# GpSimd's additions in a kernel's first stage turned into adding transfers

## The chip, the cores and the metric

The kernel runs on one core of one Trainium2 chip. The time is the device time of one launch in microseconds, lower is better. The core has five engines that run at the same time, each taking its own instructions strictly in order: TensorE (matmuls and transposes, PE in the profile, its weight loads PEld), VectorE (DVE), ScalarE (ACT), GpSimd (POOL) and SyncE (SP), which here only issues transfers. 16 DMA engines move data between HBM and the on-chip buffer SBUF; a transfer is issued from the queue of SP, of ScalarE or of GpSimd, and an instruction that needs its data waits on a semaphore until it has landed. Matmul results go to PSUM, from which DVE and ACT read them.

## What is computed

A decoder trunk of two layers on 1024 tokens of width 1024, all float32. The first layer is a gated MLP whose gate mixes tokens within chunks of 128, the second a Mamba-2 mixer. Only the beginning matters here: the RMS norm of the input, and the product of the normed tokens with the part `v` of the first layer's input weights:

```python
hn = rmsnorm(h, norm_w[i])
z, u, v = jnp.split(h @ w_in, 3, axis=-1)      # h is hn here
v = layernorm(v, ln_w, ln_b)
```

## The kernel before

**Matmuls.** A float32 value is split in a high part `hi` (rounded to float32r by ScalarE's copy) and a low part `lo` (the rest, by a subtraction on VectorE); a product is three matmuls, hi·hi, lo·hi, hi·lo (`mm3`, lines 131 to 136).

**Strassen blocks.** `Block` (from line 182) computes a product X·W with X cut in halves by tokens and by input columns (A11, A12, A21, A22) and W in four blocks `b[0,0]`, `b[1,0]`, `b[0,1]`, `b[1,1]`. Instead of eight block products there are seven, numbered 1 to 7, of sums of blocks: on the side of the tokens S1 to S4, on the side of the weights t1 = b01 − b00, t2 = b11 − t1, b11 − b01 (written over b01) and b10 − t2 (written over b10). Product 1 takes A11 and b00, 2 takes A12 and b10, 3 takes S4 and b11, 4 takes A22 and b10 − t2, 5 takes S1 and t1, 6 takes S2 and t2, 7 takes S3 and b11 − b01. A product has two units of 24 matmuls (`blk.mm(n, i)`), each for two tiles of 128 tokens; tiles 0 to 3 are token half 1, tiles 4 to 7 token half 2. `blk.post` reads a finished accumulator.

**The head.** `head` (lines 345 to 533) is the first stage. Under `manual_schedule` each engine runs its instructions in the order in which they are written. SP loads eight rows of tokens (`load_x`; row t is 128 tokens by 1024 columns, 512 KB) and the four blocks of weights (`blk.load`, 512 KB each; row 7 takes the buffer of b00 and so waits until b00 has been read for the last time). For each row ScalarE sums squares (`sq`); `rs_a` has VectorE scale them and GpSimd raise them to −1/2 (line 141); `rs_b` makes four small VectorE operations of it (lines 150 to 153); `norm` scales the row (line 376); `tr` transposes it on TensorE into PSUM; `hi` and `lo` split it into A11, A12 or A22 (lines 391 and 395), and `copy` (line 398) keeps an unsplit copy in the row's own buffer, `F[t][:, kh]` with kh the half of the columns. `yhi` and `ylo` (lines 402 and 405) split weights.

From the copies come the tokens' sums. `s3(t)`: F[t−4][:,0] −= F[t][:,0]. `s1(t)`: F[t][:,0] += F[t][:,1]. `s2(t)`: F[t][:,1] −= F[t−4][:,0] as s3 left it. `s4(t)`: F[t−4][:,1] −= F[t][:,1] as s2 left it. Of tiles 0 to 3 only the first half of the columns is copied; the second is made again from the split (`again`, hi + lo). GpSimd does the weights' four sums (lines 452, 453, 459, 460), s3 of tiles 4 to 6, s1 of tiles 4 to 6, `again`, s4 of tiles 5 to 7 and two `ylo`; GpSimd also does s3 of tile 7; VectorE does s2 of all four tiles, s1 of tile 7 and s4 of tile 4. All these are `tensor_tensor` instructions.

The products come in the order 1 and 2 of tokens half 1, unit 0; unit 1; then 4, 6, 7, 5, 3, and then the second block (`nxt`), whose weights `nxt.load` fetches into buffers as they come free, and whose sums VectorE makes. Product 3 adds onto product 5's accumulator, so it starts when `blk.post(5, ...)` has read that.

**An idiom that is there already.** `Block.add` (line 197) adds a block of weights from HBM onto a tile in SBUF by a transfer with `accum_op=ALU.add`, issued from GpSimd's queue (line 202); later blocks use it (`sums_a`, `sums_b`, `fourth`: ScalarE's `mul` by −1 at lines 211, 212, 217, 227, then adds), and line 1089 adds 512 KB from SBUF to SBUF. Two adds onto the same tile wait for one another.

Of the kernel before, what the change touches and what calls it, by code (L numbers as in the profile page):

```python
# [8 lines left out]
F32 = mybir.dt.float32  # L9
F32R = mybir.dt.float32r  # L10
AF = mybir.ActivationFunctionType
ALU = mybir.AluOpType
# [10 lines left out]
G = 8  # L23
# [6 lines left out]
def kernel(  # L30
# [21 lines left out]
    nc = tc.nc  # L52
    x = x[0]
    out = out[0]
# [22 lines left out]
    def tiny(shape, name):  # L77
        return sb.tile(shape, F32, name=name, tag="tiny", bufs=8)
# [103 lines left out]
    class Block:  # L182
# [139 lines left out]
    def v_block(gp):  # L322
        def done(name, i, a, b):
            th, j = int(name[1]) - 1, int(name[2]) - 1
            g = 2 * gp + j
            vt = k2([P, 2, 256], "vt")
            vf = vt.rearrange("p a b -> p (a b)")
            if b is None:
                nc.scalar.copy(out=vf, in_=a)
            else:  # L330
                nc.vector.tensor_tensor(out=vf, in0=a, in1=b, op=ALU.add)  # L331
            t0 = th * 4 + 2 * i
            for q in range(2):
                nc.vector.bn_stats(out=stats[:, t0 + q, g, :], in_=vt[:, q, :])
            (nc.gpsimd if gp else nc.sync).dma_start(out=v_d[g][:, t0:t0 + 2, :], in_=vt)

        def W(kh, j):
            c = 2 * DI + (2 * gp + j) * 256
            return [a_w_in[kh * 512:(kh + 1) * 512, c:c + 256]]

        return Block(HS, W, True, done)
# [3 lines left out]
    def head():  # L345

        blk = v_block(0)
        V, S, G = nc.vector, nc.scalar, nc.gpsimd
        TTv, TTg = V.tensor_tensor, G.tensor_tensor
        rows, F, TP, ss, rs = {}, {}, {}, {}, {}  # L350

        def load_x(t, dst):
# [4 lines left out]
        def sq(t):  # L357
            if t % 2 == 0:
                ss[t] = tiny([P, 8], "ss")
            junk = HS["S4"][t // 2 % 2][:, t % 2 * 2:t % 2 * 2 + 2].rearrange("p a b -> p (a b)")  # L360
            S.activation(junk, rows[t], AF.Square, accum_out=ss[t // 2 * 2][:, t % 2:t % 2 + 1])
# [24 lines left out]
        def part(name, t):  # L386
            sl = slice(t % 4 * P, (t % 4 + 1) * P)
            return [m[:, :, sl] for m in HS[name]]

        def hi(name, t, src):  # L390
            S.copy(out=part(name, t)[0], in_=src)

        def lo(name, t, src):
            h_, l_ = part(name, t)
            TTv(out=l_, in0=src, in1=h_.bitcast(F32), op=ALU.subtract)  # L395

        def copy(t, kh):
            S.copy(out=F[t][:, kh], in_=TP[t][kh])

        def yhi(n, src, eng=S.copy):  # L400
            blk.Y[n] = (wh([P, 4, 256]), wl([P, 4, 256]))
            eng(out=blk.Y[n][0], in_=src)

        def ylo(n, src, eng=TTv):
            eng(out=blk.Y[n][1], in0=src, in1=blk.Y[n][0].bitcast(F32), op=ALU.subtract)  # L405

        def again(t):

            h_, l_ = part("A12", t)
            TTg(out=F[t][:, 1], in0=h_.bitcast(F32), in1=l_.bitcast(F32), op=ALU.add)  # L410

        def s3(t):
            TTg(out=F[t - 4][:, 0], in0=F[t - 4][:, 0], in1=F[t][:, 0], op=ALU.subtract)

        def s1(t, eng):
            eng(out=F[t][:, 0], in0=F[t][:, 0], in1=F[t][:, 1], op=ALU.add)

        def s2(t):
            TTv(out=F[t][:, 1], in0=F[t][:, 1], in1=F[t - 4][:, 0], op=ALU.subtract)

        def s4(t, eng=TTg):
            eng(out=F[t - 4][:, 1], in0=F[t - 4][:, 1], in1=F[t][:, 1], op=ALU.subtract)

        b = blk.b
        t1, t2 = q4([P, 4, 256], "t1"), q4([P, 4, 256], "t2")
# [14 lines left out]
        for o, ap in ((0, a_ln_w), (16, a_ln_b), (32, b_norm_w), (48, b_conv_b)):  # L440
            n = ap.shape[1] // P
# [1 line left out]

        sq(0), sq(1), rs_a(0), rs_b(0), sq(2)
        norm(0), tr(0), norm(1), tr(1)
        hi("A11", 0, TP[0][0]), copy(0, 0), sq(3), hi("A12", 0, TP[0][1])
        rs_a(2), yhi(1, b[0, 0], V.tensor_copy)
        lo("A11", 0, TP[0][0]), ylo(1, b[0, 0]), lo("A12", 0, TP[0][1]), rs_b(2)
        hi("A11", 1, TP[1][0]), copy(1, 0), hi("A12", 1, TP[1][1])
        lo("A11", 1, TP[1][0]), lo("A12", 1, TP[1][1])  # L450
        yhi(2, b[1, 0]), ylo(2, b[1, 0])
        TTg(out=t1, in0=b[0, 1], in1=b[0, 0], op=ALU.subtract)
        TTg(out=t2, in0=b[1, 1], in1=t1, op=ALU.subtract)
        blk.mm(1, 0, False), sq(4), blk.post(1, 0), sq(5)
        blk.mm(2, 0, False)
        norm(2), tr(2), norm(3), tr(3)
        rs_a(4), rs_b(4), norm(4)
        hi("A11", 2, TP[2][0]), copy(2, 0), hi("A12", 2, TP[2][1])
        TTg(out=b[1, 0], in0=b[1, 0], in1=t2, op=ALU.subtract)
        TTg(out=b[0, 1], in0=b[1, 1], in1=b[0, 1], op=ALU.subtract)  # L460
        lo("A11", 2, TP[2][0]), lo("A12", 2, TP[2][1])
        hi("A11", 3, TP[3][0]), copy(3, 0), hi("A12", 3, TP[3][1])
        lo("A11", 3, TP[3][0]), lo("A12", 3, TP[3][1])
        norm(5)
        blk.mm(1, 1, False, (0,)), tr(4), blk.mm(1, 1, False, (1,))
        blk.mm(2, 1, False, (0,)), tr(5), blk.mm(2, 1, False, (1,))
# [2 lines left out]
        copy(4, 0), rs_a(6), blk.post(2, 0), rs_b(6)  # L469
        hi("A22", 5, TP[5][1]), copy(5, 1), copy(5, 0), blk.post(1, 1)  # L470
        lo("A22", 5, TP[5][1]), norm(6), norm(7)
        for t in (4, 5):
            s3(t), s1(t, TTg)
        yhi(6, t2)
        blk.mm(4, 0, False, (0,)), tr(6), blk.mm(4, 0, False, (1,)), tr(7)
        hi("A22", 6, TP[6][1]), copy(6, 1), copy(6, 0)
        lo("A22", 6, TP[6][1]), blk.post(2, 1), ylo(6, t2)
        hi("A22", 7, TP[7][1]), copy(7, 1), copy(7, 0)
        lo("A22", 7, TP[7][1])
        s3(6), s1(6, TTg), s3(7)  # L480
        blk.mm(4, 1, False)
        yhi(7, b[0, 1]), ylo(7, b[0, 1], TTg)
        for t in (4, 5):
            s2(t), hi("S2", t, F[t][:, 1])
        for t in (4, 5):
            lo("S2", t, F[t][:, 1])
        s2(6), hi("S2", 6, F[6][:, 1]), s1(7, TTv), s2(7), hi("S2", 7, F[7][:, 1])
        for t in (6, 7):
            lo("S2", t, F[t][:, 1])
        for t in range(4):  # L490
            again(t)
        for i in range(2):
            blk.mm(6, i, False)
        blk.post(6, 0)
# [2 lines left out]
        blk.post(6, 1), yhi(5, t1)  # L497
        for t in range(4, 8):
            lo("S3", t, F[t - 4][:, 0])
        ylo(5, t1, TTg)  # L500
        s4(4, TTv)
        for t in range(5, 8):
            s4(t)
        for i in range(2):
            blk.mm(7, i, False)
        for t in range(4, 8):
# [97 lines left out]
    for g in range(G):  # L604
# [26 lines left out]
        def mix(m, th):  # L631
            c = g * 2 + m
            mx = sm("mx")
            for q in range(4):
# [11 lines left out]
        blk = Block(HS, lambda kh, j: [a_w_in[kh * 512:(kh + 1) * 512, j * DI + g * 256:j * DI + (g + 1) * 256]],  # L646
                    False, done_zu)
# [555 lines left out]
    V = nc.vector  # L1203
# [746 lines left out]
```

## Time and profile before

| | |
|---|---|
| Time, median of 3 runs | 1601.88 us (1600.18 to 1605.85) |
| The profiled execution's own time | 1599.88 us |
| Its span in the profile | 1598.2 us |
| PE busy | 1506.0 us, 94% of the span |
| DVE, ACT, POOL busy | 1055.3, 777.0, 418.7 us |
| GpSimd's tensor instructions in the head | 4 at 2.35 to 2.38 us (weights' sums), 14 of tokens' sums (1.3 to 2.3 us), 2 low parts |

The page of the profile gives busy times by engine, the span in 40 slices, the chain that ended last and groups of instructions. Other views list instructions in order of time (start, duration, engine, line, operation, result<-inputs, shapes, count, and in brackets the idle time before and what ended it), the waits by who waited for whom, one source line or tile, or the busy times in stretches of time with the granted TensorE clock. Names are those of the program: `wr` and `t` hold weights, `wh`/`wl` their split, `hh`/`hl` the tokens' split, `xp`, `xrow` and `wr` the rows of tokens, `tp` a transposed tile in PSUM, `acc` an accumulator, `ss`, `rr`, `ru`, `rs` the norm's small tiles.

### The profile page before, as it was taken

The page shows a single profiled execution, that of the slowest core. Times are in us where ns is not written, and L with a number is a line of the kernel's source. Part 1 is how long each engine was busy: PE and PEld are TensorE (multiplying, and loading weights), DVE is VectorE, ACT ScalarE, POOL GpSimd, SP SyncE. Part 2 cuts the span into 40 slices and gives each one's busy share as a digit, 9 for nine tenths or more (in the row PEclk, how much of TensorE's full clock was granted, in tenths as well). Part 3 has the DMA queues.
Part 4 walks back from the last instruction along what each step waited for, and adds up shares of the span by engine and source line. Part 5 has one row for each costly group of instructions (what it writes and reads, how often), then busy time and mean ns, then how long its engine had stood idle before and what let it go on. Part 6 is the DMA issues. An engine that isn't in the chain of part 4 may idle for free.

```text
span 1598.2 us, 21253 instructions
## 1 busy us (share of the span) xinstructions
PE 1506.0 (94%) x7834; PEld 1239.8 (78%) x7834; DVE 1055.3 (66%) x1706; ACT 777.0 (49%) x1247; POOL 418.7 (26%) x443
## 2 busy tenths in 40 slices
PE   5799999999999999998999999989999999979988
PEld 4799988888888887876788787767777777757766
DVE  7966566666666554777637377757777767658656
ACT  4522233323222354555555455646766677544444
POOL 3601010000000131220011312126777765231231
PEclk7999999999999999999999999999999999989999
DMA  5153332332333999755367878776565665795992
GB/s 173 41 191 127 105 109 100 110 111 97 111 108 125 323 261 256 162 139 129 105 154 177 165 165 158 174 208 194 156 176 160 194 172 145 238 249 174 229 237 107
DMA packets 176919, 260.21 MB, mean 163 GB/s; under 512 B 16320, under 2 KB 102960, under 8 KB 173616
## 3 DMA queue, kind: packets, MB, share of 16 engines
q1 hardware_dynamic: 124992, 169.45, 34.3%
q0 software_dynamic: 41888, 71.58, 23.0%
q10 hardware_dynamic: 9936, 17.83, 3.1%
q8 instruction: 62, 1.02, 0.3%
q14 instruction: 41, 0.34, 0.1%
HBM read 185.61 MB, written 51.18 MB: 148 GB/s over the span
## 4 chain that ended last, share of the span: by engine, by line
PE 59%; issue 14%; DMA 9%; DVE 9%; ACT 6%; POOL 1%; ACTq 0%; SPq 0%; POOLq 0%; DVEq 0%
PE acc L136 10%; PE acc L134 9%; PE acc L135 9%; PE ab L134 4%; PE ab L136 4%; PE ab L135 4%; DMA ya<-ya 2%; PE yy L1582 2%; DMA wl<-cs_d 2%; PE yy L1586 2%; PE ao L134 2%; PE ao L135 2%; PE ao L136 2%; PE sp L1593 2%; ACT wh L111 2%
## 5 line engine op out<-in xcount | busy, mean ns | idle before, releaser
L134 PE MATMUL acc<-hh,wh 128*128 128x512 f32 x868 | 343.9, 396 | 15.4 <-ACT u L292 7.6
L136 PE MATMUL acc<-hh,wl 128*128 128x512 f32 x868 | 341.6, 394 | 1.7 <-DVE wl L112 1.6
L135 PE MATMUL acc<-hl,wh 128*128 128x512 f32 x868 | 340.8, 393 | 0.0
L134 PEld LDWEIGHTS acc<-hh,wh 128*128 128x128 f32 x868 | 164.8, 190 | 52.3 <-ACT u L292 9.3
L112 DVE TENSOR_TENSOR wl<-wr,wh 128x1024 fp32r<-128x1024 f32 (+1 forms) x99 | 118.1, 1194 | 128.2 <-ACT wh L111 128.1
L136 PEld LDWEIGHTS acc<-hh,wl 128*128 128x128 f32 x868 | 164.5, 190 | 40.2 <-DVE wl L112 5.6
L135 PEld LDWEIGHTS acc<-hl,wh 128*128 128x128 f32 x868 | 164.8, 190 | 33.4
L111 ACT CAST wh<-wr 128x1024 fp32r<-128x1024 f32 (+1 forms) x113 | 116.4, 1030 | 102.8 <-PE acc L135 57.9
L292 ACT COPY u<-acc 128x512 f32<-128x512 f32 x117 | 67.7, 583 | 197.4 <-PE acc L136 195.7
L136 PE MATMUL acc<-wh,hl 128*128 128x256 f32 x448 | 130.4, 291 | 13.2 <-DVE hl L395 13.2
L134 PE MATMUL acc<-wh,hh 128*128 128x256 f32 x448 | 131.2, 293 | 3.8 <-DVE vt L331 2.5
L135 PE MATMUL acc<-wl,hh 128*128 128x256 f32 x448 | 129.7, 290 | 1.3 <-DVE wl L405 1.3
L134 PE MATMUL ab<-hh,wh 128*128 128x512 f32 x256 | 116.5, 455 | 1.4 <-ACT zt L977 1.4
L1555 ACT ACTIVATE wl<-wl,tk 128x128 f32<-128x128 f32 x256 | 81.9, 391 | 64.1 <-DMA wl<-cs_d 63.8
L135 PE MATMUL ab<-hl,wh 128*128 128x512 f32 x256 | 101.7, 397 | 3.2 <-DVE hl L112 3.2
L136 PE MATMUL ab<-hh,wl 128*128 128x512 f32 x256 | 102.1, 399 | 0.0
L136 PEld LDWEIGHTS acc<-wh,hl 128*128 128x128 f32 x448 | 88.9, 198 | 14.3 <-DVE hl L395 14.3
L134 PEld LDWEIGHTS acc<-wh,hh 128*128 128x128 f32 x448 | 89.1, 199 | 4.8 <-issue 2.9
L134 PE MATMUL bo<-wh,xh 128*128 128x512 f32 x192 | 80.1, 417 | 12.7 <-ACT xh L111 7.4
L135 PEld LDWEIGHTS acc<-wl,hh 128*128 128x128 f32 x448 | 89.0, 199 | 1.7 <-DVE wl L405 1.5
L111 ACT CAST xh<-ya 128x1024 fp32r<-128x1024 f32 x40 | 42.0, 1050 | 90.1 <-PE ao L135 41.7
L112 DVE TENSOR_TENSOR xl<-ya,xh 128x1024 fp32r<-128x1024 f32 x40 | 49.0, 1224 | 55.8 <-ACT xh L111 55.7
(324 smaller groups left out, 3286.4 us busy)
## 6 DMA issues: line engine op xcount, KB each, us to landing
wr<-in_a_w_in_dram SPq DMA_DIRECT2D x48, 512.0 KB, 3.8
wl<-cs_d SPq DMA_DIRECT2D x64, 256.0 KB, 6.2
wr<-in_b_w_in_dram SPq DMA_DIRECT2D x30, 512.0 KB, 6.2
ya<-ya POOLq DMA_DIRECT2D x24, 512.0 KB, 15.5
wb<-in_a_w_out_dram SPq DMA_DIRECT2D x10, 1024.0 KB, 15.1
wb<-in_b_w_out_dram SPq DMA_DIRECT2D x10, 1024.0 KB, 13.7
wr<-in_b_w_in_dram SPq DMA_DIRECT2D x36, 256.0 KB, 6.7
v<-v_d SPq DMA_DIRECT2D x8, 1024.0 KB, 4.7
```

Source lines behind the costliest of these rows:

```text
L111: nc.scalar.copy(out=hi, in_=src)
L112: return (eng or nc.vector).tensor_tensor(out=lo, in0=src, in1=hi.bitcast(F32), op=ALU.subtract)
L134: nc.tensor.matmul(out=o, lhsT=l[0], rhs=r[0], start=start, stop=False, **kw)
L135: nc.tensor.matmul(out=o, lhsT=l[0], rhs=r[1], start=False, stop=False, **kw)
L136: nc.tensor.matmul(out=o, lhsT=l[1], rhs=r[0], start=False, stop=stop, **kw)
L292: nc.scalar.copy(out=self.u[n][:, i], in_=a)
L1555: nc.scalar.activation(wl[:, j, :], wl[:, j, :], AF.Relu, scale=-1.0, bias=tokc(2, c, self.g)[:, j:j + 1])
L1582: nc.tensor.matmul(out=yy[f * 64:(f + 1) * 64, pt * P:(pt + 1) * P], lhsT=w[:, j * 64:(j + 1) * 64], rhs=wl[:, j, :], start=True, stop=True)
L1586: nc.tensor.matmul(out=yy[:, 256 + pt * P:384 + pt * P], lhsT=self.state[c - 1][:, pt * P:(pt + 1) * P], rhs=self.x(3, c), start=True, sto ...
L1593: nc.tensor.matmul(out=sp[:, 0:256], lhsT=w[:, 512:640], rhs=w[:, 256:512], start=True, stop=True)
```

## The change

GpSimd keeps no tensor work in the head but the power −1/2. Tokens of half 2 (tiles 4 to 7) are copied negated, so that every sum is an addition, and the splits of S1 and S2 (`MINUS`) take the sign back (`hi` by `mul` with −1, `lo` by a `scalar_tensor_tensor`). All tiles now get copies of both halves of the columns; `again` goes. The tokens' sums of tiles 4 to 6 and s4 of tile 7 become adding transfers of 256 KB from SBUF to SBUF on GpSimd's queue; s3, s1 and s2 of tile 7 are done on VectorE. The weights' sums start from ScalarE's negated copies and add blocks of 512 KB from HBM. Both `ylo` of GpSimd go to VectorE.

```diff
         def hi(name, t, src):
-            S.copy(out=part(name, t)[0], in_=src)
+            h_ = part(name, t)[0]
+            if name in MINUS:
+                S.mul(h_, src, -1.0)
+            else:
+                S.copy(out=h_, in_=src)
         def lo(name, t, src):
             h_, l_ = part(name, t)
-            TTv(out=l_, in0=src, in1=h_.bitcast(F32), op=ALU.subtract)
+            if name in MINUS:
+                V.scalar_tensor_tensor(l_, src, -1.0, h_.bitcast(F32), ALU.mult, ALU.subtract)
+            else:
+                TTv(out=l_, in0=src, in1=h_.bitcast(F32), op=ALU.subtract)
         def copy(t, kh):
-            S.copy(out=F[t][:, kh], in_=TP[t][kh])
+            if t < 4:
+                S.copy(out=F[t][:, kh], in_=TP[t][kh])
+            else:
+                S.mul(F[t][:, kh], TP[t][kh], -1.0)
...
-        def again(t): ...
-        def s3(t): ...
-        def s1(t, eng): ...
-        def s2(t): ...
-        def s4(t, eng=TTg): ...
+        def sums(eng, *names):
+            for n, t in names:
+                a, c = {3: (F[t - 4][:, 0], F[t][:, 0]), 1: (F[t][:, 0], F[t][:, 1]),
+                        2: (F[t][:, 1], F[t - 4][:, 0]), 4: (F[t - 4][:, 1], F[t][:, 1])}[n]
+                if eng is None:
+                    nc.gpsimd.dma_start(out=a, in_=c, accum_op=ALU.add)
+                else:
+                    eng.tensor_tensor(out=a, in0=a, in1=c, op=ALU.add)
...
-        hi("A11", 0, TP[0][0]), copy(0, 0), sq(3), hi("A12", 0, TP[0][1])
+        hi("A11", 0, TP[0][0]), copy(0, 0), sq(3), hi("A12", 0, TP[0][1]), copy(0, 1)
...
-        hi("A11", 1, TP[1][0]), copy(1, 0), hi("A12", 1, TP[1][1])
+        hi("A11", 1, TP[1][0]), copy(1, 0), hi("A12", 1, TP[1][1]), copy(1, 1)
...
         yhi(2, b[1, 0]), ylo(2, b[1, 0])
-        TTg(out=t1, in0=b[0, 1], in1=b[0, 0], op=ALU.subtract)
-        TTg(out=t2, in0=b[1, 1], in1=t1, op=ALU.subtract)
+        S.mul(t2, b[0, 1], -1.0), S.mul(b[0, 1], b[0, 1], -1.0), S.mul(t1, b[0, 0], -1.0)
+        blk.add(t2, 0, 0), blk.add(b[0, 1], 1, 1), blk.add(t1, 0, 1), blk.add(t2, 1, 1)
         blk.mm(1, 0, False), sq(4), blk.post(1, 0), sq(5)
         blk.mm(2, 0, False)
         norm(2), tr(2), norm(3), tr(3)
         rs_a(4), rs_b(4), norm(4)
-        hi("A11", 2, TP[2][0]), copy(2, 0), hi("A12", 2, TP[2][1])
-        TTg(out=b[1, 0], in0=b[1, 0], in1=t2, op=ALU.subtract)
-        TTg(out=b[0, 1], in0=b[1, 1], in1=b[0, 1], op=ALU.subtract)
-        lo("A11", 2, TP[2][0]), lo("A12", 2, TP[2][1])
-        hi("A11", 3, TP[3][0]), copy(3, 0), hi("A12", 3, TP[3][1])
-        lo("A11", 3, TP[3][0]), lo("A12", 3, TP[3][1])
+        S.mul(b[1, 0], t2, -1.0), blk.add(b[1, 0], 1, 0)
+        for t in (2, 3):
+            hi("A11", t, TP[t][0]), copy(t, 0), hi("A12", t, TP[t][1]), copy(t, 1)
+            lo("A11", t, TP[t][0]), lo("A12", t, TP[t][1])
...
         lo("A22", 5, TP[5][1]), norm(6), norm(7)
-        for t in (4, 5):
-            s3(t), s1(t, TTg)
+        sums(None, (3, 4), (3, 5), (1, 4), (1, 5))
...
-        s3(6), s1(6, TTg), s3(7)
+        sums(None, (2, 4), (2, 5), (3, 6), (1, 6))
         blk.mm(4, 1, False)
-        yhi(7, b[0, 1]), ylo(7, b[0, 1], TTg)
+        sums(V, (3, 7), (1, 7), (2, 7))
+        sums(None, (2, 6), (4, 4), (4, 5))
         for t in (4, 5):
-            s2(t), hi("S2", t, F[t][:, 1])
-        for t in (4, 5):
-            lo("S2", t, F[t][:, 1])
-        s2(6), hi("S2", 6, F[6][:, 1]), s1(7, TTv), s2(7), hi("S2", 7, F[7][:, 1])
-        for t in (6, 7):
-            lo("S2", t, F[t][:, 1])
-        for t in range(4):
-            again(t)
+            hi("S2", t, F[t][:, 1]), lo("S2", t, F[t][:, 1])
+        yhi(7, b[0, 1]), ylo(7, b[0, 1])
+        for t in (7, 6):
+            hi("S2", t, F[t][:, 1]), lo("S2", t, F[t][:, 1])
+        sums(None, (4, 6), (4, 7))
...
-        ylo(5, t1, TTg)
-        s4(4, TTv)
-        for t in range(5, 8):
-            s4(t)
+        ylo(5, t1)
```

More of the change, by code (lines that the diff above doesn't have):

```diff
@@ L347, in head @@
         blk = v_block(0)
-        V, S, G = nc.vector, nc.scalar, nc.gpsimd
-        TTv, TTg = V.tensor_tensor, G.tensor_tensor
+        V, S = nc.vector, nc.scalar
+        TTv, MINUS = V.tensor_tensor, ("S1", "S2")
         rows, F, TP, ss, rs = {}, {}, {}, {}, {}
@@ L405, in ylo @@
             eng(out=blk.Y[n][1], in0=src, in1=blk.Y[n][0].bitcast(F32), op=ALU.subtract)
[L407 to L422, printed above, removed]
+        def sums(eng, *names):
[6 more added lines that the diff above has]
+                    eng.tensor_tensor(out=a, in0=a, in1=c, op=ALU.add)
         b = blk.b
```

## The prediction

> **What bounds the kernel now.** Read in this order: the page's busy times, the busy times by stretch, the waits of the first 130 us, and the engines' instructions in order of time.
>
> ```profile
> PE 1506.0 (94%) x7834; PEld 1239.8 (78%) x7834; DVE 1055.3 (66%) x1706; ACT 777.0 (49%) x1247; POOL 418.7 (26%) x443
> ```
> ```profile
> 66.19:83.10 16.91, 14.41 (x118) 14.23 (x119) 15.65 (x17) 12.47 (x20) 7.53 (x4) 1.00 0.17 51
> 83.10:150.00 66.90, 66.89 (x544) 65.56 (x545) 47.22 (x81) 17.76 (x24) 8.93 (x15) 1.00 0.51 171
> ```
> ```profile
> PE acc L136 <- DVE hl L395: 13.2, 5, 3.9
> ```
>
> The columns of the second row are PE, PEld, DVE, ACT and POOL busy, the granted clock, the DMA share and GB/s. TensorE is busy for 94% of the span, and in the stretch from 83.10 us it is busy without a break. The change ends there, so its whole effect is the time at which product 3 of the first block starts (83.11 us), against now. Before it TensorE waits, 13.2 us in five waits for low parts from VectorE. Of the waits these decide, the last one for VectorE's reading of an accumulator (2.50 us, in brackets):
>
> ```profile
> 34.16 0.58 PE L136 MATMUL acc<-wh,hl 128*128 128x256 f32 x1 [3.89 <-DVE hl L395]
> 66.19 0.38 PE L136 MATMUL acc<-wh,hl 128*128 128x256 f32 x1 [1.66 <-DVE hl L395]
> 83.11 0.35 PE L134 MATMUL acc<-wh,hh 128*128 128x256 f32 x1 [2.50 <-DVE vt L331]
> ```
>
> The three places are unit 1 of product 1 (34.16), tile 6 of product 6 (66.19) and product 3 (83.11). VectorE is late partly because its instructions grow while GpSimd has a tensor instruction:
>
> ```profile
> 8.06 0.16 DVE L150 TENSOR_TENSOR ru<-rr 128x2 f32<-128x2 f32 x1 [0.83 <-POOL rr L141]
> 27.00 2.33 DVE L150 TENSOR_TENSOR ru<-rr 128x2 f32<-128x2 f32 x1 [0.81 <-POOL rr L141]
> 71.21 5.90 DVE L395 TENSOR_TENSOR hl<-xrow,hh 128x512 fp32r<-128x512 f32 x3 [0.89 <-ACT hh L391]
> 79.87 2.48 DVE L395 TENSOR_TENSOR hl<-xp,hh 128x512 fp32r<-128x512 f32 x4
> ```
>
> A 0.16 us operation takes 2.33 us; a low part costs 2.0 us (5.90 for three) instead of 0.6 (2.48 for four). This goes, and with it 4 us of low parts of S1. In exchange every sum becomes a transfer with a latency.
>
> **Step 1, the weights' sums, up to unit 1.** ScalarE reaches `mul` of t2 after `yhi(2)`, which two new copies push back, and after b01 has landed.
>
> ```profile
> 4.97 11.05 DMA wr<-in_a_w_in_dram
> 15.15 1.09 ACT L402 CAST wh<-wr 128x1024 fp32r<-128x1024 f32 x1
> 28.75 0.59 ACT L391 CAST hh<-tp 128x512 fp32r<-128x512 f32 x1 [2.79 <-PE tp L382]
> 29.23 0.59 ACT L398 COPY xp<-tp 128x512 f32<-128x512 f32 x1
> L211 ACT ACTIVATE t<-wr x7: 634/1059/1060, 707.9 to 998.9; 128x1024 f32<-128x1024 f32 x6, 128x512 f32<-128x512 f32 x1
> ```
>
> Copies follow each other every 0.48 us, so `yhi(2)` runs from 16.1 to 17.2 us, after b01 (16.0); the `mul` takes 1.06, and the first add goes out at 18.2. Prices of an add come from later in this trace: one 512 KB add from HBM with nothing beside it, one from SBUF, and what the DMA engines move meanwhile:
>
> ```profile
> DMA to landing us min/median/max: 5.9/5.9/5.9
> ```
> ```profile
> DMA to landing us min/median/max: 5.0/5.0/5.0
> ```
> ```profile
> 798.00:801.00 3.00, 3.00 (x15) 2.45 (x15) 1.42 (x2) 2.97 (x4) 0.00 (x0) 1.00 1.22 193
> 16.50:19.91 3.41, 2.14 (x11) 1.85 (x9) 3.34 (x3) 1.05 (x2) 3.33 (x2) 0.50 1.03 403
> ```
>
> Adds stream at 193 GB/s, plain loads at 403: 512 KB cost 2.7 and 1.3 us of streaming. Four adds share one queue, and the fourth (t2 += b11) stands behind three: it lands at 18.2 + 5.9 + 3·2.7 = 32.2. Row 7, whose load waits for the last `mul`, falls into them; I take half of its 1.3 us: 32.9. The far bound of this case is the same group of four from line 202 later, beside other transfers:
>
> ```profile
> 709.25 1.33 POOL L202 DMA_DIRECT2D t<-in_b_w_in_dram  x1 [1.40 <-ACT t L211]
> 710.35 1.54 POOL L202 DMA_DIRECT2D wr<-in_b_w_in_dram  x1
> ```
> ```profile
> L202 POOL DMA_DIRECT2D t<-in_b_w_in_dram x2: 1270/1284/1297, 714.8 to 716.3; - x2
> DMA to landing us min/median/max: 7.9/8.9/9.9
> ```
>
> From 709.3 to 716.3 + 9.9 it took 16.9 us, hence 35.1; the near bound, row 7 at nothing, is 32.2. ScalarE meets `mul` of b10 from t2 before the splits of tile 2, so these and the copies queue behind it, and TensorE waits for them: 32.9 + 1.06, high part 0.59, low part 0.69, and unit 1 starts at 35.2 instead of 34.16. So the relief of `rs_b` (2.2 us for each operation that GpSimd stretched) is lost: a ScalarE wait takes the place of the VectorE stall. Under its cover lie, on GpSimd, the power for rows 4 and 5, which stands behind the fourth add's wait for the first (18.2 + 5.9), and on VectorE the `rs_b` and norm behind that, done by 29; without the cover they would hold tile 2 until then. On SP row 7 and the small loads behind it move some 1.5 us; nothing needs them before 41. The copies of tiles 2 and 3 end before `yhi(4)` can begin; alone they would cost ScalarE 4·0.48.
>
> [...]
>
> **Step 2, up to the first token sum.** The b10 add goes out at 34.0 and lands at 39.9. `yhi(4)` waits on it; behind it on ScalarE stand the split and copy of tile 4, two squares and `copy(4,0)`:
>
> ```profile
> 38.51 1.07 ACT L361 ACTIVATE hl<-xrow 128x1024 fp32r<-128x1024 f32 x1
> 40.99 0.70 POOL L141 TENSOR_TENSOR rr<-ss,mhalf 128x2 f32<-128x2 f32 x1 [9.36 <-DVE ss L365]
> ```
>
> 39.9 + 1.0 + 2·0.5 + 2·1.07 + 0.5 = 44.5; GpSimd's queue has the power (0.70, after the squares) first, so s3 of tile 4 goes out at 44.9, of tile 5 at 46.0. The norms of rows 6 and 7, freed of GpSimd's interference, come about where they did; products 2 and 4 hide the rest.
>
> **Step 3, the tokens' chain.** Of a 256 KB add from SBUF there is no row. Half the stream off 5.0 gives 3.6; a plain 256 KB store lands in 2.6, plus 0.7 for the slower stream 3.3; under load one took 6.4.
>
> ```profile
> DMA to landing us min/median/max: 2.6/3.2/3.9
> ```
> ```profile
> DMA to landing us min/median/max: 6.4/6.4/6.4
> ```
> ```profile
> 23.00:42.00 19.00, 15.11 (x91) 14.90 (x90) 16.36 (x25) 9.34 (x18) 6.37 (x5) 0.72 0.04 0
> 52.00:55.20 3.20, 1.94 (x16) 1.74 (x16) 3.20 (x3) 1.71 (x4) 3.20 (x3) 1.00 0.71 202
> ```
>
> I take 3.5, near the two quiet rows, and 1.1 between issues (709.25 to 710.35). Each sum reads what the one before wrote, or overwrites what it read, and GpSimd's queue holds all behind a waiting one: s3 of tile 5 lands 49.5, s1 53.0, s2 goes out at 53.0; behind it s3 of tile 6 at 54.1, lands 57.6; s1 61.1; s2 64.6. Two loads of the next block's weights (512 KB each; the last row has one, DMA share 0.71) fall in: half of 2·1.3, and 0.2 for hops, gives 66.1. High part 0.59, low part 0.69: tile 6 of product 6 starts at 67.4 instead of 66.19. The three sums of tile 7 on VectorE (0.6 each) and the two `ylo` that it takes over (1.2 each) lie in its own waits for these landings and beside product 7; the s4 adds, queued behind s2 of tile 6, land by 72 and product 3 needs them at 83.
>
> **Step 4, to product 3.** TensorE idles from about 60 us, and the clock follows:
>
> ```profile
> 33.56:36.97 3.41, 2.81 (x13) 2.82 (x14) 3.41 (x6) 0.00 (x0) 0.00 (x0) 0.50 0.05 0
> 36.97:40.39 3.42, 3.42 (x18) 3.42 (x17) 2.07 (x3) 2.84 (x5) 0.00 (x0) 0.50 0.05 0
> 60.87:64.28 3.41, 3.41 (x18) 3.29 (x16) 3.41 (x3) 0.62 (x1) 3.39 (x3) 0.50 0.00 0
> 62.09 0.41 PE L135 MATMUL acc<-wl,hh 128*128 128x256 f32 x1
> 62.31 0.41 PE L136 MATMUL acc<-wh,hl 128*128 128x256 f32 x1
> 67.24 0.28 PE L135 MATMUL acc<-wl,hh 128*128 128x256 f32 x1
> 67.36 0.28 PE L136 MATMUL acc<-wh,hl 128*128 128x256 f32 x1
> ```
>
> It changes at steps of 3.41 us; 2.81 busy us in one did not raise it, a full one did. So it is half from 64.28 to 71.1: a matmul every 0.21 instead of 0.12. Of 120 matmuls (unit 1 of 6, all of 7 and 5) 17.6 run by 71.1; 102.4·0.12 = 12.3 follow: product 3 could start at 83.4. The 2.5 us stall is gone, since the low parts of S1 lose their 4 us and VectorE reads product 5's accumulator in time. So 83.4 against 83.11: **+0.3 us**. The profiled execution, 1599.88 us, becomes 1600.2; the median of before is 2.0 above it, so I say 1602.2.
>
> Bounds of this case: row 7 and the loads costing nothing and 3.3 per add start tile 6 at 64.2, the clock rises at 67.7, and product 3 starts 2.9 us early: 1599. With 35.1, 3.6 and full loads it starts 4.1 us late or somewhat more: 1606.
>
> **Rivals.** *Slower: the four adds under load.* Place: ScalarE's `mul` of b10. A second such group took from 794.0 to 802.5 + 13.0, 21.5 us:
>
> ```profile
> L202 POOL DMA_DIRECT2D t<-in_b_w_in_dram x1: 1292/1292/1292, 794.0 to 794.0; - x1
> L202 POOL DMA_DIRECT2D t<-in_b_w_in_dram x2: 1272/1542/1812, 801.7 to 802.5; - x2
> DMA to landing us min/median/max: 8.3/10.6/13.0
> ```
>
> Then t2 lands at 39.7, 6.8 later, and everything behind it: 1609. It decides once t2 lands after 37.4 (4.5 later). For it: row 7 and many small loads share the engines then. Against: from 23 to 42 us the small loads take 0.04 of them (row above). *Faster: adds stream like plain loads.* Then a 512 KB add lands in 4.5, t2 at about 27 and unit 1 starts 5 us early; the six token adds save up to 0.7 each: 5 to 9 us, 1593 to 1597. The adds' own row at 193 GB/s speaks against it. [...] *The change does not free VectorE:* if issuing adds slows VectorE as tensor work does, the 2.5 us stall stays: 1604.4, same by the bound below. No row here decides it; all the stretched VectorE rows stand beside GpSimd's tensor work.
>
> **How the numbers follow.** A measurement of this kernel can tell some 0.3% (4.8 us) from no change. Forecast 0.50, slower rival 0.28, faster rival 0.14, no relief 0.08. Faster 0.14, same 0.50 + 0.08 = 0.58, slower 0.28. The forecast's own range is 1599 to 1606; to leave out no more than 2 in 10 the slower rival's side is taken in: 1598 to 1609.5. A token add at 6.4 throughout (+17) is left out, since little else moves then.
>
> **What would show it.** Right: a long ScalarE wait for t2's landing ahead of tile 2's high part, unit 1 near 35; VectorE's `rs_b` at 0.16 us each; token adds landing in about 3.5 us; half clock from 64 to 71; no wait ahead of product 3, near 83.4. Wrong: t2 landed before 30 or after 37, tile 6 of product 6 off 67.4 by more than 4 us, or a stall after 83.

## The result and the profile after

The changed kernel takes 1618.3 us (median of 6 runs, 1612.77 to 1625.7), the kernel before 1601.29 (6 runs, 1598.2 to 1605.85). The ratio is 1.0112, with a 95% interval of 1.0081 to 1.0142. Slower by 1.1%: the forecast was 1602.2, and its range ended at 1609.5. The profiled execution took 1612.77 us, with a span of 1611.1.

The first page of the profile after, busy times:

```profile
PE 1505.2 (93%) x7834; PEld 1240.1 (77%) x7834; DVE 1031.9 (64%) x1705; ACT 782.7 (49%) x1255; POOL 399.2 (25%) x441
```

VectorE's busy time fell by 23.4 us and GpSimd's by 19.5, and TensorE does the same work. What got longer is idle time in the head. Busy times by stretch, after (columns as before: PE, PEld, DVE, ACT, POOL, granted clock, DMA share, GB/s):

```profile
66.19:83.10 16.91, 8.45 (x47) 7.76 (x45) 5.88 (x8) 4.56 (x10) 5.79 (x8) 0.76 0.80 165
83.10:100.00 16.90, 16.83 (x119) 16.61 (x120) 11.82 (x18) 11.22 (x20) 1.36 (x2) 0.84 0.50 118
100.20:167.10 66.90, 66.90 (x547) 65.56 (x545) 46.77 (x79) 18.82 (x25) 8.74 (x15) 1.00 0.50 166
```

The stretch in which TensorE is busy without a break began at 83.1 us before; now it begins some 17 us later, and in the 17 us ahead of 83.1 TensorE is busy for 8.45 where it was busy for 14.41. How far the whole work has moved is read most exactly from an instruction of the second block, ScalarE's copy of an accumulator, in the instructions in order of time, before and then after:

```profile
103.53 0.58 ACT L292 COPY u<-acc 128x512 f32<-128x512 f32 x1 [1.78 <-PE acc L136]
```
```profile
120.59 0.59 ACT L292 COPY u<-acc 128x512 f32<-128x512 f32 x1 [1.79 <-PE acc L136]
```

It is 17.06 us late. This copy is the measure of every run below, since it leaves out the later stages, which vary from run to run (it is read from one profiled execution of each run): at the end the two profiled executions differ by 12.9 us (1612.77 against 1599.88), the medians by 17.0. Of the waits of the first 105 us of the changed kernel these bear on the loss (engine and line, whom it waited for, us in total, times, longest):

```profile
ACT wr L462 <- DMA t<-in_a_w_in_dram: 13.7, 1, 13.7
PE acc L134 <- ACT hh L395: 12.8, 1, 12.8
ACT hh L393 <- DMA xrow<-xp: 12.3, 3, 6.9
ACT wh L413 <- DMA wr<-in_a_w_in_dram: 11.7, 1, 11.7
```

ScalarE waits three times for adds: for t2 (L462, the `mul` of b10), for b10 (L413, `yhi(4)`) and for the tokens' sums (L393, a high part of a sum). TensorE's own waits hang behind these. TensorE's instructions after, those that follow a wait:

```profile
37.68 0.58 PE L134 MATMUL acc<-wh,hh 128*128 128x256 f32 x1 [12.85 <-ACT hh L395]
38.90 0.58 PE L136 MATMUL acc<-wh,hl 128*128 128x256 f32 x1 [0.41 <-DVE hl L402]
55.69 0.58 PE L134 MATMUL acc<-wh,hh 128*128 128x256 f32 x1 [6.84 <-DVE hl L402]
...
72.82 0.58 PE L134 MATMUL acc<-wh,hh 128*128 128x256 f32 x1 [3.94 <-ACT hh L393]
83.17 0.58 PE L134 MATMUL acc<-wh,hh 128*128 128x256 f32 x1 [4.58 <-ACT hh L393]
```

The last row is the start of tile 6 of product 6 (its first hi·lo matmul comes at 83.89 us, 66.19 before). No row behind it, up to 105 us, has a wait: the 2.50 us stall ahead of product 3 is gone. The first row, unit 1 of product 1, stands behind the longest wait, but its first hi·lo matmul (second row) comes only 4.7 us later than before (34.16): TensorE got to this point earlier than before, and waited there then too. What the kernel before does not have is ScalarE's wait of 11.7 us for b10, which shows on TensorE as the wait in the middle, and its cause is a single transfer. Line 202's adds, t2's fourth and b10's, by the view of one source line (duration of the issue, its time, and the time to landing):

```profile
L202 POOL DMA_DIRECT2D t<-in_a_w_in_dram x1: 1270/1270/1270, 24.5 to 24.5; - x1
DMA to landing us min/median/max: 11.5/11.5/11.5
...
L202 POOL DMA_DIRECT2D wr<-in_a_w_in_dram x1: 1305/1305/1305, 37.5 to 37.5; - x1
DMA to landing us min/median/max: 15.3/15.3/15.3
```

The add of b10 was alone on GpSimd's queue and took 15.3 us instead of 5.9. The view of the DMA queues shows what went on meanwhile, for 38.8 to 46 us and for 46 to 53 us (q0 is GpSimd's queue, q1 SyncE's; pieces, MB, share of the 16 engines' time):

```profile
q1 hardware_dynamic: 754, 0.00, 4.6%
...
q0 software_dynamic: 528, 0.52, 47.4%
q1 hardware_dynamic: 291, 0.00, 1.9%
```

In the first 7.2 us the add moves nothing at all, although the engines are busy for 4.6% only. On SyncE's queue 754 pieces go by that hold next to no data. The same view of the kernel before, 23 to 42 us, tells what they are:

```profile
q1 hardware_dynamic: 1888, 0.01, 4.4%
...
dsk<-in_b_d_skip_dram SPq DMA_DIRECT2D x2, 4.0 KB
```

`dsk` is a table for the last layer, loaded early by two transfers. Each takes 16 single floats, every second one, to 64 partitions: 1024 pieces of 4 bytes. In both kernels these two loads drip through for over 20 us, from their issue at 24.2 us to about 45 before, from 25.7 to about 49 after. Before, no engine waits for a transfer in that time.

### The profile page after: what moved, and what is told of

Same layout as the page of the kernel before. It is cut to its first block, busy times and chain, and to the rows that moved or that the text cites. A ratio compares the mean times of both kernels' runs of the same rounds, so it can differ in the third digit from the quotient of the medians.

```text
span 1611.1 us, 21278 instructions
## 1 busy us (share of the span) xinstructions
PE 1505.2 (93%) x7834; PEld 1240.1 (77%) x7834; DVE 1031.9 (64%) x1705; ACT 782.7 (49%) x1255; POOL 399.2 (25%) x441
## 4 chain that ended last, share of the span: by engine, by line
PE 55%; issue 14%; DMA 9%; DVE 9%; ACT 6%; SPq 1%; POOL 1%; ACTq 0%; POOLq 0%; DVEq 0%
PE acc L136 9%; PE acc L134 9%; PE acc L135 9%; DMA wl<-cs_d 4%; PE ab L134 3%; PE ab L136 3%; PE ab L135 3%; DMA ya<-ya 2%; PE yy L1578 2%; PE yy L1582 2%; DVE wl L112 2%; PE bo L135 2%; PE ao L134 2%; PE ao L135 2%; PE ao L136 2%
```

## Experiments

The theory from these rows: an add that goes out while such small pieces are queued is held until they are through, and that is most of the 17 us. The rivals: the adds are slow in the head for another reason (the other loads there, adds behind each other), or the tokens' sums are to blame. All runs, each with the ratio of its time to that of the kernel before from the same chip, and the measuring copy's distance from 103.53 in the profiled execution:

| Run | Time, us (runs) | Ratio, 95% interval | Copy, us |
|---|---|---|---|
| changed kernel | 1618.3 (6) | 1.0112 [1.0081, 1.0142] | +17.06 |
| e1 wide small load | 1606.4 (10) | 1.0035 [1.002, 1.0049] | +7.69 |
| e2 the same, in the kernel before | 1599.65 (10) | 1.0001 [0.9986, 1.0016] | −0.10 |
| e3 tokens' sums alone | 1604.23 (6) | 1.0032 [1.0017, 1.0048] | +3.81 |
| e4 weights' sums alone | 1617.19 (4) | 1.0107 [1.0082, 1.0133] | +19.43 |
| e5 wide load, next loads late | 1605.72 (10) | 1.0037 [1.0018, 1.0056] | +6.02 |
| e6 tokens' sums alone, wide, late | 1599.38 (10) | 1.0001 [0.9984, 1.0019] | −2.33 |
| e7 small load twice | 1624.07 (2) | 1.0147 [1.0108, 1.0185] | +26.78 |
| e8 e5 with the weights' order changed | 1600.57 (12) | 1.0001 [0.9982, 1.0021] | −1.27 |
| e9 small load late | 1617.98 (4) | 1.0114 [1.0079, 1.015] | +18.75 |
| e10 small load on ScalarE's queue | 1616.95 (4) | 1.0105 [1.0076, 1.0133] | +16.95 |
| e11 the kernel before, wide, late | 1603.2 (12) | 1.003 [1.0016, 1.0044] | +4.62 |

### e1 and e2: the small load in wide pieces

```diff
-    dskv = b_d_skip[0].rearrange("(c f) -> f c", f=2)
+    dskw = cst.tile([P, 16, 2], F32, name="dskw")
+    nc.sync.dma_start(out=dskw.rearrange("p c f -> p (c f)"), in_=b_d_skip[0].partition_broadcast(P))
     for f in range(2):
-        nc.sync.dma_start(out=dsk[f * 64:(f + 1) * 64, :], in_=dskv[f].partition_broadcast(64))
+        nc.vector.tensor_copy(out=dsk[f * 64:(f + 1) * 64, :], in_=dskw[f * 64:(f + 1) * 64, :, f])
```

> The changed kernel with one edit: the load of b_d_skip, 2048 pieces of 4 bytes, becomes one load of 128 pieces of 128 bytes and two tiny VectorE copies. Theory S (a newly issued add waits in the DMA engines until the stream of small pieces has drained): the b10 add, 15.3 us from issue to landing in the changed kernel, lands within 7 us; t2's last add lands by 34 instead of 36.0; tile 6 of product 6 starts near 67 to 70 instead of 83.2, and the whole is some 13 to 16 us faster than the changed kernel, within 4 us of the kernel before. Rival D (an add that finds its queue empty, or one that reads HBM here, is that slow by itself): the b10 add still takes over 12 us, and the time stays within 4 us of the changed kernel.

> The kernel before with the same edit of the b_d_skip load. It issues no add while the small pieces run, so both theories expect no change: product 3 at 83.1 within 0.5 us, the time within 0.3% of the kernel before. Were it faster, the small load would cost the kernel before something that neither theory names.

In e1, line 202's view for t2's fourth add and b10's add:

```profile
L202 POOL DMA_DIRECT2D t<-in_a_w_in_dram x1: 1270/1270/1270, 24.8 to 24.8; - x1
DMA to landing us min/median/max: 10.1/10.1/10.1
...
L202 POOL DMA_DIRECT2D wr<-in_a_w_in_dram x1: 1305/1305/1305, 36.3 to 36.3; - x1
DMA to landing us min/median/max: 6.0/6.0/6.0
```

The add of b10 takes 6.0 us instead of 15.3, and 9.4 of the 17.06 us are gone with one load that has nothing to do with the change. In the kernel before the same edit does nothing (e2, the copy 0.10 us earlier), since no adds are there to be held. But 7.7 us remain, where I had expected at most 4: the small pieces are the larger part, not the whole. Part of the rest shows in the tokens' adds of e1, s1 of tile 5 and s2 of tile 4, once a store and the first load of the next block's weights go out beside them:

```profile
L424 POOL DMA_DIRECT2D xrow<-xrow x1: 846/846/846, 53.1 to 53.1; - x1
L424 POOL DMA_DIRECT2D xrow<-xp x1: 843/843/843, 55.2 to 55.2; - x1
DMA to landing us min/median/max: 6.5/6.5/6.5
```

These two adds took 6.5 us each, where the first one, at 47.4 us, took 3.5.

### e7, e9, e10: which pieces hold an add

Three edits of the changed kernel leave the small load in its 4-byte form and change its number, its time or its queue. e7 loads the table twice:

```diff
     for f in range(2):
         nc.sync.dma_start(out=dsk[f * 64:(f + 1) * 64, :], in_=dskv[f].partition_broadcast(64))
+    dskx = cst.tile([P, 16], F32, name="dskx")
+    for f in range(2):
+        nc.sync.dma_start(out=dskx[f * 64:(f + 1) * 64, :], in_=dskv[f].partition_broadcast(64))
```

> The changed kernel with the load of b_d_skip in 4-byte pieces made twice (4096 pieces, the second copy unused). Theory S: the stream of small pieces lasts some 19 us longer (to about 68), and the b10 add lands near 72 instead of 52.7; the time is 17 to 20 us above the changed kernel. Rival D (the small pieces are not what holds it): the b10 add lands at 52 to 55, the time is that of the changed kernel.

b10's add, SyncE's issues of the two added loads, and the queues from 38.8 to 56 us:

```profile
L202 POOL DMA_DIRECT2D wr<-in_a_w_in_dram x1: 1305/1305/1305, 37.4 to 37.4; - x1
DMA to landing us min/median/max: 25.5/25.5/25.5
```
```profile
L596 SPq DMA_DIRECT2D dskx<-in_b_d_skip_dram x2: 4625/8058/11492, 28.2 to 32.9; - x2
```
```profile
q1 hardware_dynamic: 1844, 0.01, 4.7%
```

The add is held for 10.2 us more, and in 17 us nothing of it moves. 10.2 us is the price of one more load of 1024 pieces (1844 pass in 17.2 us, so by estimate 1024 in 9.6), not of the two that were added, so the expected step was twice too large. The issues say why: the last small load needed 11.5 us to be issued, until 44.4 us, so it was handed over after the add (done at 38.7) and did not hold it. The copy moves by 9.7 us against the changed kernel, the time by 5.8 (two runs).

e9 issues the two loads from SyncE behind the next block's loads (86 us), in the same form:

```diff
+        dskv = b_d_skip[0].rearrange("(c f) -> f c", f=2)
+        for f in range(2):
+            nc.sync.dma_start(out=dsk[f * 64:(f + 1) * 64, :], in_=dskv[f].partition_broadcast(64))
         nxt.prep(1)
         for i in range(2):
             blk.mm(3, i, False)
```

> The changed kernel with the two loads of b_d_skip (2048 pieces of 4 bytes) in the same form, but issued after the loads of the next block's weights, behind product 5 of the first block, instead of at 25.7 us. Theory (an add is held by those small loads that were handed over before it, whatever is handed over later): with nothing small handed over ahead of them after 25 us, t2's fourth add lands at about 34.9 instead of 36.0 and b10's add takes about 6 us instead of 15.3, as in the run with the load in wide pieces; the head ends about 8 us after the kernel before's and the time is about 1606, against 1618. Now the pieces drain some 20 us from about 85 us on, where no add is waited for: at most 2 us more if they hold the loads that the second block waits for. Rival (it was the wide pieces themselves, or a transfer of another kind, that made the add quick): b10's add still takes over 10 us and the time stays at 1615 or more.

```profile
L202 POOL DMA_DIRECT2D wr<-in_a_w_in_dram x1: 1305/1305/1305, 36.6 to 36.6; - x1
DMA to landing us min/median/max: 5.9/5.9/5.9
```
```profile
109.32 0.69 DVE L331 TENSOR_TENSOR vt<-acc,u 128x512 f32<-128x512 f32 x1 [11.40 <-DMA v_d<-vt]
```

Half of it came as expected: b10's add takes 5.9 us, so the form of the pieces was not at fault, only what is queued ahead of an add. The time did not follow. Now the pieces stand ahead of the stores of finished `v` on the same queue; VectorE waits 11.40 us until such a store has landed and frees its buffer, and TensorE waits behind it (6.8 us for ScalarE's split weights). I had allowed at most 2 us for that: the pieces hold other transfers issued behind them on the same queue too, here plain stores, not adds alone.

e10 issues them from ScalarE's queue, behind the squares of tile 5, at 20.4 and 21.4 us:

```diff
         blk.mm(1, 0, False), sq(4), blk.post(1, 0), sq(5)
+        dskv = b_d_skip[0].rearrange("(c f) -> f c", f=2)
+        for f in range(2):
+            nc.scalar.dma_start(out=dsk[f * 64:(f + 1) * 64, :], in_=dskv[f].partition_broadcast(64))
         blk.mm(2, 0, False)
```

> The changed kernel with the two loads of b_d_skip in the same form, issued by ScalarE (its own queue) behind the squares of tile 5, at about 22 to 24 us, ahead of t2's fourth add (24.5 us), instead of by SyncE at 25.7 us, behind it. Theory (an add is held by small loads handed over before it, on whatever queue): now the fourth add is the one that is held, as where it went out 0.05 us behind the first of these loads and took 18.1 us: t2 lands at 41 to 44 instead of 36.0, the add of b10 goes out at 43 to 45 and takes 6 to 9 us, landing about where it did (50 to 53); the time is 1612 to 1620. Rival (only pieces on SyncE's queue hold the adds): t2 lands at about 35, b10's add takes about 6 us, and the time is about 1606.

```profile
L202 POOL DMA_DIRECT2D t<-in_a_w_in_dram x1: 1270/1270/1270, 24.8 to 24.8; - x1
DMA to landing us min/median/max: 17.8/17.8/17.8
...
L202 POOL DMA_DIRECT2D wr<-in_a_w_in_dram x1: 1305/1305/1305, 44.0 to 44.0; - x1
DMA to landing us min/median/max: 9.0/9.0/9.0
```

Now t2's fourth add, which goes out behind them, is the slow one: 17.8 us instead of 11.5, and b10's takes 9.0. The third add, issued at 20.4 us between the two loads, is late too (16.1 us instead of 11.8). The sum of the fourth and b10's is what it was. So in these runs it does not matter on which of the two queues the pieces are; it matters that they were handed over first.

### e3 and e4: the two halves of the change alone

e3 leaves the weights' sums on GpSimd as tensor work and turns only the tokens' sums into adds; e4 is the kernel before with the weights' sums as adds (the lines that the diff removes, at the same places). The diff is that of e3 against the changed kernel.

```diff
-        S.mul(t2, b[0, 1], -1.0), S.mul(b[0, 1], b[0, 1], -1.0), S.mul(t1, b[0, 0], -1.0)
-        blk.add(t2, 0, 0), blk.add(b[0, 1], 1, 1), blk.add(t1, 0, 1), blk.add(t2, 1, 1)
+        TTg(out=t1, in0=b[0, 1], in1=b[0, 0], op=ALU.subtract)
+        TTg(out=t2, in0=b[1, 1], in1=t1, op=ALU.subtract)
...
-        S.mul(b[1, 0], t2, -1.0), blk.add(b[1, 0], 1, 0)
+        TTg(out=b[1, 0], in0=b[1, 0], in1=t2, op=ALU.subtract)
+        TTg(out=b[0, 1], in0=b[1, 1], in1=b[0, 1], op=ALU.subtract)
```

> The changed kernel with the four weights' sums put back on GpSimd as before; only the tokens' sums are adding transfers. Theory S (the loss lies in the weights' adds; a token add lands in 3.3 to 3.8 us): the first token add goes out near 41 to 42 instead of 57.8, tile 6 of product 6 starts near 64 to 66, product 3 at 80 to 82, 1 to 3 us before the 83.1 of the kernel before. Rival T (the tokens' serial adds cost as much): product 3 at 86 or later, the time at least 4 us above the kernel before.

> The kernel before with only the weights' sums as ScalarE's negations and adds; the tokens' sums stay as they were on GpSimd and VectorE. Theory S: t2's last add lands at 35 to 36 and the b10 add 14 to 16 us after its issue, near 52; product 3 starts at 98 to 102, and the time is 15 to 18 us above the kernel before. Rival T (the loss lies in the tokens' part): the time is within 5 us of the kernel before.

e3, the first token add:

```profile
L424 POOL DMA_DIRECT2D xp<-xrow x1: 1032/1032/1032, 41.7 to 41.7; - x1
DMA to landing us min/median/max: 6.9/6.9/6.9
```

It goes out 16 us earlier than in the changed kernel and so falls into the small pieces: 6.9 us instead of 3.5; e3 ends 3.81 us late. By its numbers that is what the rival of this run had said, a loss of 4 us or more by the tokens' adds themselves; e6, below, speaks against it. e4, t2's fourth add, and TensorE ahead of product 3:

```profile
L202 POOL DMA_DIRECT2D t<-in_a_w_in_dram x1: 1270/1270/1270, 25.1 to 25.1; - x1
DMA to landing us min/median/max: 18.1/18.1/18.1
```
```profile
101.12 0.55 PE L134 MATMUL acc<-wh,hh 128*128 128x256 f32 x1 [2.48 <-DVE vt L331]
```

The adds of the weights alone cost as much as the whole change, 19.43 us. Here SyncE issues the first small load at 25.06 us, 0.05 ahead of the fourth add, where in the changed kernel it came 1.1 us behind it: t2 takes 18.1 us instead of 11.5, and b10's add 8.9 instead of 15.3; I had expected the slow one to be b10's again. The fourth add is not held still here. Between 31 and 43 us, with the third add landed at 31.1, GpSimd's queue (q0) moves 0.47 MB of it among the small pieces, by estimate 2.4 us of work at the 193 GB/s of adds alone:

```profile
q0 software_dynamic: 477, 0.47, 27.1%
q1 hardware_dynamic: 1241, 0.00, 5.0%
```

So the pieces delay an add in two ways: b10's add in the changed kernel moved nothing for 7.2 us, t2's here crept along between them. The stall ahead of product 3 stays, 2.48 us; where the tokens' sums leave GpSimd it goes. The two halves do not add up (19.4 + 3.8 against 17.1): they wait for the same pieces, and a later start of the second half finds them gone (the first token add of the changed kernel, at 57.8 us, took 3.5).

### e5, e6, e8 and e11: what is left without the small pieces

e5 adds to e1 that the next block's loads go out after product 5, from ScalarE's queue. e6 is e3 with both aids. e11 is the kernel before with both, as the control of e6.

```diff
         for kh, j in ((0, 0), (1, 0), (0, 1), (1, 1)):
-            nxt.load(kh, j)
+            nxt.b[kh, j] = wr([P, 4, 256])
+            nc.scalar.dma_start(out=nxt.b[kh, j], in_=nxt.W(kh, j)[0].rearrange("(k p) n -> p k n", p=P))
```

e8 is e5 with b10's `mul` and add behind the splits of tiles 2 and 3 and the first of tile 4, and its split behind the tokens' copies:

```diff
-        S.mul(b[1, 0], t2, -1.0), blk.add(b[1, 0], 1, 0)
...
-        yhi(4, b[1, 0]), hi("A22", 4, TP[4][1]), copy(4, 1), sq(6), sq(7)
-        ylo(4, b[1, 0]), lo("A22", 4, TP[4][1])
+        hi("A22", 4, TP[4][1]), copy(4, 1)
+        S.mul(b[1, 0], t2, -1.0), blk.add(b[1, 0], 1, 0), sq(6), sq(7)
+        lo("A22", 4, TP[4][1])
...
-        hi("A22", 5, TP[5][1]), copy(5, 1), copy(5, 0), blk.post(1, 1)
-        lo("A22", 5, TP[5][1]), norm(6), norm(7)
+        hi("A22", 5, TP[5][1]), copy(5, 1), copy(5, 0)
+        norm(6), lo("A22", 5, TP[5][1]), norm(7)
+        yhi(4, b[1, 0]), blk.post(1, 1), ylo(4, b[1, 0])
```

> The changed kernel with the wide load of b_d_skip, and with the four loads of the next block's weights issued from ScalarE's queue after product 5 instead of from SP's as their buffers come free. Theory S, widened (any transfers already queued hold a newly issued add, so the two adds that took 6.5 us beside these loads land in 3.3 to 3.8 without them): the s2 add of tile 6 lands 2.5 to 3.5 us earlier than with the wide load alone (72.9), and the time is some 3 us lower than with the wide load alone, provided that the late loads are not waited for. Rival H (those adds were slow for their place in the chain): no add gets faster, and the time stays where the wide load alone left it or rises.

> Only the tokens' sums as adds (weights' sums on GpSimd as before), with the wide small load and the late loads of the next block. Theory S: the first token add, 6.9 us with the small pieces in flight, lands in 3.3 to 3.8; the s2 add of tile 6 lands near 63 instead of 69.6; product 3 starts at 80 to 82; the time is 1 to 4 us below the kernel before, so not distinguishable from it by 0.3%. Rival T (the tokens' serial adds are a loss in themselves): the time stays 4 us or more above the kernel before.

> As with the wide load and the late loads of the next block, and with ScalarE's order changed: the negation of b10 behind the split of tile 4 instead of ahead of tile 2's, and the split of b10 behind the copies of tiles 4 and 5. Theory S together with the prediction's step 1 (ScalarE's wait for t2 holds unit 1, and its wait for b10 holds the first token add): unit 1 starts near 30 instead of 36.6, the first token add goes out near 39 to 41 instead of 47.4, product 3 starts at 78 to 81, and the time is 2 to 5 us below the kernel before. Rival V (VectorE or the order of products holds unit 1 and the tokens once ScalarE is free): product 3 at 82 or later, the time not below the kernel before.

> The kernel before with the two aids alone: b_d_skip loaded in wide pieces, and the next block's loads issued from ScalarE's queue after product 5. It is the control for the run with the tokens' sums as adds and both aids, whose copy of product 7 of the second stretch starts at 101.20 instead of 103.53 us. Theory (the 2.3 us come from the freed VectorE: the 2.5 us stall ahead of product 3 goes): here nothing frees VectorE, the stall of about 2.5 us ahead of product 3 stays, that copy starts at 103.0 to 103.6, and the time is that of the kernel before within 0.2%. Rival (the aids themselves gave the 2.3 us): the stall shrinks and the copy starts near 101.

e5, the same two adds, s1 of tile 5 and s2 of tile 4, now without loads beside them:

```profile
L424 POOL DMA_DIRECT2D xrow<-xrow x1: 846/846/846, 54.7 to 54.7; - x1
DMA to landing us min/median/max: 3.8/3.8/3.8
...
L424 POOL DMA_DIRECT2D xrow<-xp x1: 843/843/843, 56.9 to 56.9; - x1
DMA to landing us min/median/max: 3.5/3.5/3.5
```

The two adds that took 6.5 us take 3.8 and 3.5, so the loads were the reason. The chain from the first token add to the landing of s2 of tile 6 takes 22.4 us instead of 25.5 in e1, but it begins 1.7 us later: b10's add took 7.5 us in e5, with nothing seen beside it, and why is open. So the head gains only 1.7 us (6.02 against 7.69), and the time does not tell e5 from e1. With the order of e8 other work covers the waits for t2 and b10 too (the first token add goes out at 39.8 us instead of 49.1), and of the loss nothing is left. TensorE's first instruction of product 3 in e8 and in e6:

```profile
81.83 0.36 PE L134 MATMUL acc<-wh,hh 128*128 128x256 f32 x1 [0.34 <-DVE vt L331]
```
```profile
80.77 0.35 PE L134 MATMUL acc<-wh,hh 128*128 128x256 f32 x1 [0.34 <-DVE vt L331]
```

Product 3 starts at 81.83 and 80.77 us, against 83.11 before. Both are ahead of the kernel before in the head, by 1.27 and 2.33 us, and by their times (ratio 1.0001 for both) neither can be told from it; the 2 to 5 us that I had expected of e8 did not come. No version that beats it measurably came out.

The control e11 missed its expectation. Its stall ahead of product 3 did not stay at 2.5 us but grew, and ScalarE shows why:

```profile
85.47 0.55 PE L134 MATMUL acc<-wh,hh 128*128 128x256 f32 x1 [3.69 <-DVE vt L331]
```
```profile
81.57 0.62 ACT L391 CAST hh<-xp 128x512 fp32r<-128x512 f32 x1 [4.92 <-DVE wl L405]
```

The moved loads stand in ScalarE's queue and wait there for buffers that come free only when VectorE has read the old weights; the splits of S4 behind them wait 4.92 us. With VectorE freed, as in e6, the buffers are free in time and ScalarE loses 1.57 us. So the aids alone gave nothing: the wide load changes nothing by itself (e2), and the late loads cost here. That the 2.33 us of e6 come from the freed VectorE fits this, but it is not shown: e11 is no clean control, since its own edit costs 4.62 us.

## Why the prediction was wrong

Step by step, forecast against the changed kernel and e1 (a landing is the issue plus its time to landing, from the rows above or from their view of the same line):

| | Forecast | Changed kernel | e1, no small pieces |
|---|---|---|---|
| t2's fourth add landed | 32.9 | 36.0 | 34.9 |
| b10's add goes out | 34.0 | 37.5 | 36.3 |
| its time to landing | 5.9 | 15.3 | 6.0 |
| first token add goes out | 44.9 | 57.8 | 47.4 |
| s2 of tile 6 landed | 66.1 | 82.5 | 72.9 |
| first hi·lo matmul of tile 6 of product 6 | 67.4 | 83.9 | 74.3 |

**Step 1, t2: place right, size low.** ScalarE does wait at the `mul` of b10 for t2, and TensorE behind it. t2 lands 3.1 us later than said and 0.9 behind the far bound of 35.1, though within the 37 that was named as a sign of being wrong; unit 1's first hi·lo matmul, said for 35.2, comes at 38.9. By e1 the small pieces make 1.1 of the 3.1 us (t2 lands at 34.9 without them, 35.2 in e9); the other 2 are there without them, with row 7 and the remaining small loads beside the four adds. Which of these takes them was not tried.

**Step 2, b10: the step that failed.** "The b10 add goes out at 34.0 and lands at 39.9" took the price of an add with nothing beside it. It was 15.3 us: 9.4 of the 16.4 us by which s2 of tile 6 landed late. The information was there: the slower rival named the many small loads, and was set aside with "from 23 to 42 us the small loads take 0.04 of them". That row was read rightly and told the wrong thing. Here the share of engine time did not tell whether another transfer got through (4.6% while b10's add moved nothing for 7.2 us); the count of pieces in the queues' view (1888 in 19 us) would at least have raised the question.

**The slower rival** came nearest (adds that are slow beside other transfers, 1609), but had the wrong transfer: it wanted t2 after 37.4, t2 came at 36.0, and the add behind it was the one that was held. The faster rival is out: adds did not stream like plain loads. It had 4.5 us for an add of 512 KB; the traces of e1 and e9 show 6.0 and 5.9 with nothing small beside it.

**Between b10 and the tokens:** from the landing to the first token add 5.1 us (52.7 to 57.8), forecast 5.0. Right.

**Step 3, the tokens' chain: price right, surroundings low.** Without loads beside them (e5) the token adds up to s2 of tile 6 took 3.3 to 4.0 us, and one issued 0.5 us behind another 4.7; the forecast was 3.5. The chain from the first issue to the landing of s2 of tile 6 took 24.7 us instead of 21.2. e1 and e5 show that the next block's loads cost single adds about 3 us each (6.5 against 3.8 and 3.5), where 1.3 us was put in for all of them.

**Step 4 and VectorE.** The relief came as said. VectorE's instructions after, an `rs_b` operation and three low parts of S1 (2.33 and 5.90 us before):

```profile
26.55 0.16 DVE L150 TENSOR_TENSOR ru<-rr 128x2 f32<-128x2 f32 x1 [3.90 <-POOL rr L141]
...
91.63 1.89 DVE L400 SCALAR_TENSOR_TENSOR hl<-xrow,hh 128x512 fp32r<-128x512 f32 x3
```

Issuing adds did not slow VectorE: its low part (L402) at 38.15 us took 0.69 us beside the b10 add's issue (37.45 to 38.75). So the rival in which it does is out (its time should have read 1604.7, 1602.2 + 2.5, not 1604.4), and the 2.50 us stall went. e4 and e3 place it with the tokens' sums: it stays where they are tensor work. From that hi·lo matmul of tile 6 (83.89) to product 3 (100.2, by the stretches above) it took 16.3 us, forecast 16.0; the granted clock was 0.84 in the mean of 83.10 to 100.00, 0.50 from 83.10 to 88.65 and 1.00 from there on, so TensorE ran at half clock for 5.55 of these 16.9 us, against the 3.7 us of the forecast.

The added errors are 3.1 (t2), 0.4 (`mul` to issue), 9.4 (b10), 0.1 and 3.5 (chain) = 16.5 us at the landing of s2 of tile 6; from there to tile 6's first hi·lo matmul it took 1.4 us instead of 1.3, and to product 3 0.3 us more than forecast. The large ones have one sign: the adds were priced as almost undisturbed, with 0.7 us put in for row 7 and 1.3 for the next block's loads.

**What stays open.** Why a DMA engine that is idle for 95% of the time lets an add wait behind 4-byte pieces of another queue is not shown. Nor is it shown why b10's add moved nothing at all until they were nearly through, while t2's in e4 moved between them. That they delay an add (15.3 us against 6.0 and 5.9), that those handed over ahead of it count (e7, e9), and that either queue will do (e10), is.

## What to carry to other kernels

Before a wait is turned into a transfer, list every transfer that is handed over ahead of it, with its number of pieces: here a load of 4 KB in 4-byte pieces cost the add behind it about 10 us (e7), with the DMA engines 95% idle, and it was harmless only while nobody waited behind it (e2). Moving the load moved the damage (e9, e10); giving it wide pieces removed it (e1, the add at 6.0 us). A chain of short sums that becomes a chain of transfers pays the latency at each link (3.3 to 4.0 us for 256 KB, e5); here it broke even only where other work covered the links (e8) or where only the tokens' sums were turned and other loads stayed out of the way (e6).

## What the runs showed of the hardware

- 1024 pieces of 4 bytes pass in about 9.6 us by estimate (1844 in 17.2 us, e7), and an add of 512 KB handed over behind them on another queue takes 15.3 us behind two such loads (the changed kernel), 25.5 behind three (e7), and 5.9 (e9), 6.0 (e1) and 7.5 (e5) behind none. Pieces of two queues can pass in the same stretch: 477 of GpSimd's and 1241 of SyncE's in 12 us (e4). For b10's add in e7 it was not so: in 17.2 us 1844 pieces pass and nothing of the add, which had been issued before. Whether the add's own pieces already stood with the engines is not shown.
- The issue slowed down too: with two such loads under way, SyncE needed 4.6 and 11.5 us to issue two more (e7), where the first two took 0.7 and 1.0.
- A 256 KB add from SBUF to SBUF took 3.3 to 4.0 us with no load beside it (e5; one issued 0.5 us behind another add took 4.7), and 6.5 beside one load of 512 KB and one store of 256 KB (e1).
